# Gathers that convert float32 rows to float16 on the way, in place of a ScalarE cast, in a gather, cumulative-sum and matmul kernel

## The chip, the cores and the metric

The kernel runs on one core of a Trainium2 chip. The metric is the device time of one execution in microseconds (us); medians of several executions are quoted, and fast runs are compared with fast runs. The kernel before takes 349.65 us in the median (348.95 to 350.15, 4 runs).

## The reference, cut to what matters

```python
B, S, N, D = (16, 4096, 2048, 512)        # x: (B, S, D) float32, indices: (B, N) sorted, w: (D, D)
gathered = x[b_idx, indices, :].copy()
cs = np.cumsum(gathered, axis=1)
return np.matmul(cs, w).astype(np.float32)
```

16 x 2048 gathered rows of 2 KB are 67.1 MB read, the output is 67.1 MB written. The kernel works in 256 tiles of 128 rows. For each tile TensorE multiplies the gathered rows with a triangle of ones (the sums, turned so that D, the length of a row, lies on the partitions), VectorE adds the last column of the tile before (the carry), TensorE multiplies with w (the projection), ScalarE drains PSUM to SBUF, and SyncE stores four tiles (1 MB) at a time.

## The kernel before

Gathers are issued by GpSimd, one tile each, into a ring of 16 float32 slots. ScalarE casts them to float16 into a second ring (8 pairs), up to 6 tiles ahead of the drains, and in between drains the projections:

```python
    def gather(t):
        g, r = divmod(t, R)
        if t >= NG:                                        # NG = 16 slots; freed by the casts
            pool.need(s_c, cast_by[R * (g + 1) - NG - 1])
        ...
        nc.gpsimd.indirect_dma_start(
            out=g32[g % (NG // R)][:, r, :],               # float32 slot
            out_offset=None,
            in_=x_flat,
            in_offset=bass.IndirectOffsetOnAxis(ap=ap, axis=0),
            element_offset=(t // NT) * S * D,
        ).then_inc(s_g[t % NG], 16)

    def cast(t, n, first=None):                            # ScalarE
        g, r = divmod(t, R)
        for u in range(t, t + n):
            act.need(s_g[u % NG], 16 * (u // NG + 1), first)
        nc.scalar.copy(
            out=g16[g % NH][:, r : r + n], in_=g32[g % (NG // R)][:, r : r + n]
        ).then_inc(s_c, 1)

    def sums(t, u, first=None):                            # TensorE
        ...
        pe.need(s_c, cast_by[t] if first is None else cast_by[2 * U + t] - 2 * U // R, first)
        ...
            mm = nc.tensor.matmul(
                out=pa[t % NA][:, c],
                lhsT=g16[g % NH][:, r, c * P : (c + 1) * P],
                rhs=uq[:] if first is None and g in PLAIN else ut[:],
                start=(c == 0), stop=(c == DC - 1),
            )
    ...
    def step(u, first=None):                               # ScalarE's program
        ...
        for t, n in casts[u if first is None else 2 * U + u]:
            cast(t if first is None else t - 2 * U, n, first)
        drain(u, first)
```

Of the kernel before, what the change touches and what calls it, by code (L numbers as in the profile page):

```python
# [7 lines left out]
P = 128  # L8
FP32 = mybir.dt.float32
FP16 = mybir.dt.float16  # L10
# [23 lines left out]
def kernel(  # L34
# [7 lines left out]
    nc = tc.nc  # L42

    B, S, D = x.shape
    N = indices.shape[1]
    R = 2
# [3 lines left out]
    T = B * NT  # L50
    G = T // R
# [1 line left out]
    KI = T // P  # L53
    FIRST = 2 * R
    NG = 16
    LEAD = 3
    FAR = 6
    NH = 8
    NA = 4
    NB = 4  # L60
    NC = 4
    W = 2
    H = 1
    NO = 4
    U = NT
    V = max(U, W * R * NO)
    assert V % U == 0 and V % (W * R * NO) == 0 and T % V == 0 and U % NG == 0 and U % NA == 0 and U % (R * NC) == 0 and U % NB == 0
    assert D == 512 and N % (R * P) == 0 and T % P == 0

    x_flat = x.rearrange("b s d -> (b s) d")  # L70
# [1 line left out]
    const = ctx.enter_context(tc.tile_pool(name="const", bufs=1))  # L72
# [8 lines left out]
    ut = const.tile([P, R, Q], FP16)  # L81
    uq = const.tile([P, P], FP16)
    ident = const.tile([P, P], FP32)
    zeros = const.tile([P, D], FP16)
    spare = const.tile([P, 1], FP16)
    g32 = [const.tile([P, R, D], FP32, name=f"g32_{i}") for i in range(NG // R)]
    g16 = [const.tile([P, R, D], FP16, name=f"g16_{i}") for i in range(NH)]
    cst = [const.tile([P, DC, R, P], FP16, name=f"cst{i}") for i in range(NC)]
    ob = [const.tile([P, W, R, D], FP32, name=f"ob{i}") for i in range(NO)]
    pa = [ps.tile([P, DC, R, Q], FP32, name=f"pa{i}") for i in range(NA)]  # L90
# [4 lines left out]
    def sem(name):  # L95
        return tc.alloc_semaphore(name)

    s_z, s_ut, s_wc, s_if, s_pt, s_prep, s_of, s_c = (
        sem(f"s_{n}") for n in ("z", "ut", "wc", "if", "pt", "prep", "of", "c")
    )  # L100
# [1 line left out]
    s_w = [sem(f"s_w{c}") for c in range(DC)]  # L102
    s_idx = [sem(f"s_idx{k}") for k in range(KI)]
    s_ol = sem("s_ol")
    s_g = [sem(f"s_g{i}") for i in range(NG)]
    s_o = [sem(f"s_o{i}") for i in range(NO)]
    s_a = sem("s_a")
    s_d = sem("s_d")
    s_b = sem("s_b")
    s_e = sem("s_e")  # L110

    pool, pe, dve, act, sp = (
        Lane(e) for e in (nc.gpsimd, nc.tensor, nc.vector, nc.scalar, nc.sync)
    )

    casts = []
    cast_by = []
    for u in range(T):
        far = min(FAR, 2 if u < R else 3 + (u + 4) // 8, 3 + (T - 1 - u) // 6)
        casts.append([])  # L120
        while len(cast_by) <= min(u + far, T - 1):
            n = R if far > 5 and len(cast_by) % R == 0 else 1
            casts[u].append((len(cast_by), n))
            cast_by += [cast_by[-1] + 1 if cast_by else 1] * n

    for u in range(2 * U + U, T - 2 * U):
        assert casts[u] == [(t + U, n) for t, n in casts[u - U]]

    def gather(t):
        g, r = divmod(t, R)  # L130
        if t >= NG:
            pool.need(s_c, cast_by[R * (g + 1) - NG - 1])
        if t < FIRST:
            pool.need(s_first[g], 16)
            ap = idx_first[:, t, 0:1]
        else:
            pool.need(s_prep, t // P + 1)
            ap = idxg[:, t // P, t % P : t % P + 1]
        nc.gpsimd.indirect_dma_start(  # L139
            out=g32[g % (NG // R)][:, r, :],  # L140
            out_offset=None,
            in_=x_flat,
            in_offset=bass.IndirectOffsetOnAxis(ap=ap, axis=0),
            element_offset=(t // NT) * S * D,
        ).then_inc(s_g[t % NG], 16)


    PLAIN = (0, 1, G - 2, G - 1)

    def cast(t, n, first=None):  # L150
        g, r = divmod(t, R)
        for u in range(t, t + n):
            act.need(s_g[u % NG], 16 * (u // NG + 1), first)
        nc.scalar.copy(  # L154
            out=g16[g % NH][:, r : r + n], in_=g32[g % (NG // R)][:, r : r + n]
        ).then_inc(s_c, 1)

    def sums(t, u, first=None):
        g, r = divmod(t, R)
        tiles = None if first is None else R * first  # L160
        pe.need(s_c, cast_by[t] if first is None else cast_by[2 * U + t] - 2 * U // R, first)
        pe.need(s_d, t - NA + 1, tiles)
        for c in range(DC):
            if c == 1 and u is not None:
                pe.need(s_e, u - NB + 1, tiles)
            mm = nc.tensor.matmul(  # L166
                out=pa[t % NA][:, c],
                lhsT=g16[g % NH][:, r, c * P : (c + 1) * P],
                rhs=uq[:] if first is None and g in PLAIN else ut[:],
                start=(c == 0),  # L170
                stop=(c == DC - 1),
            )
        mm.then_inc(s_a, 1)
# [28 lines left out]
    def project(u, t, first=None):  # L202
        g, j = divmod(u, R)
        tiles = None if first is None else R * first
        pe.need(s_e, u - NB + 1, tiles)
        pe.need(s_d, u + 1 if first is None and g in PLAIN else R * (g + 1), tiles)
        for c in range(DC):
            if c == 2 and t is not None:
                pe.need(s_d, t - NA + 1, tiles)
            mm = nc.tensor.matmul(  # L210
                out=pb[u % NB][:],
                lhsT=cst[g % NC][:, c, j, :],
                rhs=w16[:, c, :],
                start=(c == 0),
                stop=(c == DC - 1),
            )
        mm.then_inc(s_b, 1)
# [6 lines left out]
    def store(g, n):  # L224
        b, h = divmod(g, GB)
        rows = out[b, h * R * P : (h + n) * R * P, :]
        src = ob[g // W % NO]
        if g in (0, G - 1):
            for j in range(R):
                sp.need(s_e, R * g + j + 1)  # L230
                nc.sync.dma_start(
                    out=rows[j * P : (j + 1) * P, :], in_=src[:, g % W, j]
                ).then_inc(s_ol if g else (s_o[0], s_of)[j >= H], 16)
            return
        sp.need(s_e, R * (g + n))
        order = "(g j p) d -> p g j d" if g in PLAIN else "(g p j) d -> p g j d"
        rows = rows.rearrange(order, p=P, j=R)
        src = src[:, g % W : g % W + n]
        if n < W:
            done = s_ol if g >= W else (s_o[0], s_of)[R + g > H]  # L240
            nc.sync.dma_start(out=rows, in_=src).then_inc(done, 16)
            return
        for i in range(H):
            part = slice(i * P // H, (i + 1) * P // H)
            nc.sync.dma_start(out=rows[part], in_=src[part]).then_inc(s_o[g // W % NO], 16)


    with nc.allow_non_contiguous_dma(reason="a few indices, one per partition"):
        for k, eng in enumerate((nc.sync, nc.scalar)):
            t = k * R  # L250
            eng.dma_start(
                out=idx_first[:, t : t + R, :],
                in_=indices[0, t * P : (t + R) * P]
# [4 lines left out]
    for k in range(KI):  # L258
        nc.sync.dma_start(
            out=idx64[:, k, :], in_=idx_rows[k * P : (k + 1) * P, :]  # L260
# [8 lines left out]
    for g in range(G - W, G):  # L269
        store(g, 1)  # L270
    for i in range(G // W - NO, G // W - 1):
        sp.need(s_o[i % NO], 16 * H * (i // NO + 1))
    sp.need(s_ol, 16 * (R + W - 1))


# [4 lines left out]
        out=ident[:],  # L280
        in_=ident[:],
# [7 lines left out]
        out=ut[:],  # L289
        in_=ut[:],  # L290
# [9 lines left out]
        out=uq[:],  # L300
        in_=uq[:],
# [23 lines left out]
    for k in range(KI):  # L325
# [3 lines left out]
            out=pb[k % NB][:, :P], in_=idxf[:, k, :], identity=ident[:]  # L329
# [20 lines left out]
    order = []  # L350
    done = 0
# [7 lines left out]

    head = order.index((False, 2 * U - 1)) + 1  # L360
    tail = order.index((False, T - 2 * U - 1)) + 1
    step = 2 * U
    for i in range(head + step, tail):
        assert order[i] == (order[i - step][0], order[i - step][1] + U)

    def run(i, first=None):
        is_sums, t = order[i]
        after = next((v for k, v in order[i + 1 :] if k != is_sums), None)
        if first is not None:
            t -= 2 * U  # L370
            after -= 2 * U
        if is_sums:
            sums(t, after, first)
        else:
            pe.need(s_wc, DC)
            project(t, after, first)

    for i in range(head):
        run(i)
    with nc.tensor.Fori(2 * U // R, (T - 2 * U) // R, U // R) as first:  # L380
        pe.new_pass()
        for i in range(head, head + step):
            run(i, first)
# [7 lines left out]
        act.need(s_w[c], 16)  # L391
        nc.scalar.copy(out=w16[:, c, :], in_=w32[:, c, :]).then_inc(s_wc, 1)  # L392
    def step(u, first=None):
        if first is None and u == min(W * R * NO, 2 * U - 1):
            act.need(s_of, 16 * (R + W - 1 - H))
        if u % (W * R) == 0:
            stored = first if first is None else first * (16 * H) // (R * W * NO)
            act.need(s_o[u // R // W % NO], 16 * H * (u // R // W // NO), stored)
        for t, n in casts[u if first is None else 2 * U + u]:
            cast(t if first is None else t - 2 * U, n, first)  # L400
        drain(u, first)


    for u in range(2 * U):
        step(u)
    with nc.scalar.Fori(2 * U, T - 2 * U, V) as first:
        act.new_pass()
        for u in range(V):
            step(u, first)
    for u in range(T - 2 * U, T):  # L410
        step(u)
# [30 lines left out]
```

## Time and profile before

| | us |
|---|---|
| kernel before, timed, median of 4 runs | 349.65 |
| span of the profile that the prediction had | 439.2 |
| span of a second profile of the same kernel, taken later on another execution | 348.4 |

The profile was of an execution that took a quarter longer than the timed ones. A busy row of the page gives an engine's busy time and share; the DMA row gives, in tenths, how busy the 16 DMA engines were in each fortieth of the span; a queue's share is the time of its packets over 16 engines' span.

### The profile page before, as it was taken

Reading aid. Unit: us, or ns where it says so; the run is one execution under the profiler, and the core shown is the slowest. Engines: PE = TensorE matmul, PEld = TensorE weight load, DVE = VectorE, ACT = ScalarE, POOL = GpSimd, SP = SyncE. Lnnn points to the kernel's source line nnn. Section 1 sums busy time; section 2 is a strip of 40 time slices with the busy share of each in tenths; the row PEclk is TensorE's granted clock in tenths of the full one; section 3 lists DMA queues with packets and bytes.
Section 4 is the critical chain, followed back from the end, with each engine's and each line's share of the span. In section 5 each row is a group of like instructions: output and inputs, shape, how many; then the busy total and the mean of one; then the engine's idle time right before and its main releaser. Section 6 shows DMA issues by size and latency. Waiting matters only on the chain.

```text
span 439.2 us, 6408 instructions
## 1 busy us (share of the span) xinstructions
PE 329.8 (75%) x2066; PEld 171.5 (39%) x2066; DVE 178.4 (41%) x263; ACT 263.6 (60%) x407; POOL 243.7 (55%) x266
## 2 busy tenths in 40 slices
PE   6518687777877786679787697768777697876995
PEld 2203343343434343335344353434334343443552
DVE  2104343444344444345344344344345353543552
ACT  4216566556665665576656575566576666665794
POOL 6764557565655566556565465565555665655300
PEclk9756989798989899988899698996989969998898
DMA  7864979799888999989898899988989999999966
GB/s 225 256 212 156 347 273 344 252 336 364 285 318 304 333 351 328 350 294 339 316 353 295 310 336 335 359 318 273 366 310 328 331 337 328 300 330 349 331 242 241
DMA packets 39884, 135.68 MB, mean 309 GB/s; under 512 B 5825, under 2 KB 6081, under 8 KB 39873
## 3 DMA queue, kind: packets, MB, share of 16 engines
q0 software_dynamic: 20480, 67.13, 47.9%
q1 hardware_dynamic: 18832, 67.90, 38.9%
q10 hardware_dynamic: 560, 0.53, 0.4%
q8 instruction: 5, 0.08, 0.1%
q14 instruction: 7, 0.05, 0.0%
HBM read 68.42 MB, written 67.11 MB: 309 GB/s over the span
## 4 chain that ended last, share of the span: by engine, by line
PE 74%; issue 10%; DVE 7%; another core or an unknown queue 7%; ACT 1%; DVEq 0%; ACTq 0%; SPq 0%
PE pb L210 55%; PE pa L166 18%; DVE cst L198 7%; PE pb L316 1%; DVE cst L185 0%; ACT ob L222 0%; ACT g L154 0%; PE pb L328 0%; DVEq L26 0%; DVE zeros L320 0%; DVEq L437 0%; ACTq L26 0%; SPq L93 0%
## 5 line engine op out<-in xcount | busy, mean ns | idle before, releaser
L210 PE MATMUL pb<-w,cst 128*128 128x512 f16 x1024 | 293.1, 414 | 84.7 <-DVE cst L198 60.1
L139 POOL DMA_INDIRECT g<-in_x_dram,idxg x252 | 238.2, 945 | 165.1 <-ACT g L154 97.6
L198 DVE TENSOR_TENSOR cst<-pa,cst 128x512 f16<-128x512 f32 x240 | 166.1, 692 | 231.3 <-PE pa L166 162.2
L222 ACT COPY ob<-pb 128x512 f32<-128x512 f32 x256 | 146.2, 591 | 164.6 <-PE pb L210 108.1
L210 PEld LDWEIGHTS pb<-w,cst 128*128 128x128 f16 x1024 | 94.3, 104 | 164.9 <-DVE cst L198 65.8
L154 ACT CAST g<-g 128x1024 f16<-128x1024 f32 (+1 forms) x147 | 138.4, 945 | 0.3 <-issue 0.2
L166 PE MATMUL pa<-ut,g 128*128 128x128 f16 x992 | 103.9, 230 | 16.0 <-issue 12.8
L166 PEld LDWEIGHTS pa<-ut,g 128*128 128x128 f16 x992 | 81.5, 104 | 87.7 <-issue 33.8
L185 DVE CAST cst<-pa 128x512 f16<-128x512 f32 x16 | 11.0, 686 | 16.2 <-PE pa L166 12.6
L316 PE MATMUL pb<-zeros 128*128 128x512 f16 x16 | 5.9, 538 | 1.5 <-DVE zeros L320 1.5
L139 POOL DMA_INDIRECT g<-in_x_dram,idx_first x4 | 4.0, 994 | 1.6 <-issue 0.9
L166 PE MATMUL pa<-uq,g 128*128 128x128 f16 x32 | 3.1, 219 | 1.9 <-issue 1.8
L166 PEld LDWEIGHTS pa<-uq,g 128*128 128x128 f16 x32 | 2.2, 97 | 4.2 <-issue 3.1
L316 PEld LDWEIGHTS pb<-zeros 128*128 128x128 f16 x16 | 2.1, 135 | 4.2 <-issue 2.2
L392 ACT CAST w<-w 128x512 f16<-128x512 f32 x2 | 1.1, 616 | 3.4 <-DMA w<-in_w_dram 3.4
L389 ACT ACT_TABLE_LOAD x1 | 1.3, 1283 | 2.5 <-issue 2.5
L323 DVE CAST idxf<-idx 128x128 f32<-128x128 uint32 x2 | 0.5, 227 | 3.8 <-DMA idx<-in_indices_dram 3.8
L337 DVE CAST w<-w 128x512 f16<-128x512 f32 x2 | 0.8, 422 | 1.6 <-DMA w<-in_w_dram 1.6
L328 PE MATMUL pb<-ident,idxf 128*128 128x128 f32 x2 | 0.9, 447 | 0.0
L328 PEld LDWEIGHTS pb<-ident,idxf 128*128 128x128 f32 x2 | 0.4, 206 | 0.9 <-issue 0.9
L320 DVE MEMSET zeros<- 128x256 uint32 x1 | 0.3, 272 | 1.1 <-SPq L93 1.1
L334 DVE CAST idxg<-pb 128x128 uint32<-128x128 f32 x2 | 0.6, 292 | 0.3 <-PE pb L328 0.2
(11 smaller groups left out, 2.1 us busy)
## 6 DMA issues: line engine op xcount, KB each, us to landing
out_dram<-ob SPq DMA_DIRECT2D x62, 1024.0 KB
g<-in_x_dram,idxg POOLq DMA_INDIRECT x252
out_dram<-ob SPq DMA_DIRECT2D x4, 256.0 KB, 2.8
out_dram<-ob SPq DMA_DIRECT2D x2, 512.0 KB, 3.4
w<-in_w_dram ACTq DMA_DIRECT2D x2, 256.0 KB, 3.3
w<-in_w_dram SPq DMA_DIRECT2D x2, 256.0 KB
idx<-in_indices_dram SPq DMA_DIRECT2D x2, 128.0 KB, 2.6
g<-in_x_dram,idx_first POOLq DMA_INDIRECT x4
```

Source lines behind the costliest of these rows:

```text
L139: nc.gpsimd.indirect_dma_start(out=g32[g % (NG // R)][:, r, :], out_offset=None, in_=x_flat, in_offset=bass.IndirectOffsetOnAxis(ap=ap, ax ...
L154: nc.scalar.copy(out=g16[g % NH][:, r : r + n], in_=g32[g % (NG // R)][:, r : r + n]).then_inc(s_c, 1)
L166: mm = nc.tensor.matmul(out=pa[t % NA][:, c], lhsT=g16[g % NH][:, r, c * P : (c + 1) * P], rhs=uq[:] if first is None and g in PLAIN else ...
L185: nc.vector.tensor_copy(out=dst, in_=src).then_inc(s_d, 1)
L198: nc.vector.tensor_tensor(out=dst, in0=src, in1=last, op=mybir.AluOpType.add).then_inc(s_d, 1)
L210: mm = nc.tensor.matmul(out=pb[u % NB][:], lhsT=cst[g % NC][:, c, j, :], rhs=w16[:, c, :], start=(c == 0), stop=(c == DC - 1),)
L222: nc.scalar.copy(out=ob[g // W % NO][:, g % W, j], in_=pb[u % NB][:]).then_inc(s_e, 1)
L316: nc.tensor.matmul(out=pb[NB - 1][:], lhsT=zeros[:, :P], rhs=zeros[:], start=True, stop=True)
L328: nc.tensor.transpose(out=pb[k % NB][:, :P], in_=idxf[:, k, :], identity=ident[:]).then_inc(s_pt, 1)
L337: nc.vector.tensor_copy(out=w16[:, c, :], in_=w32[:, c, :]).then_inc(s_wc, 1)
L389: nc.scalar.copy(out=spare[:], in_=zeros[:, :1])
L392: nc.scalar.copy(out=w16[:, c, :], in_=w32[:, c, :]).then_inc(s_wc, 1)
```

## The change

The intent is to take the cast off ScalarE: GpSimd's gathers write float16 directly, the sums read the gathers' slots, and the slots are freed by the sums. The core of the diff (the rest reworks how waits are counted in TensorE's loop, which is now 32 tiles long, and strips parameters whose value was 1):

```diff
-    LEAD = 3
-    FAR = 6
-    NH = 8
+    NS = 32
+    FREE = 2
+    LEAD = 4
...
-    g32 = [const.tile([P, R, D], FP32, name=f"g32_{i}") for i in range(NG // R)]
-    g16 = [const.tile([P, R, D], FP16, name=f"g16_{i}") for i in range(NH)]
+    g16 = [const.tile([P, R, D], FP16, name=f"g16_{i}") for i in range(NG // R)]
...
-        if t >= NG:
-            pool.need(s_c, cast_by[R * (g + 1) - NG - 1])
+        if t % FREE == 0:
+            pool.need(s_a, t + FREE - NG)
...
-            out=g32[g % (NG // R)][:, r, :],
+            out=g16[g % (NG // R)][:, r, :],
...
-    def cast(t, n, first=None):
-        ...
-        pe.need(s_c, cast_by[t] if first is None else cast_by[2 * U + t] - 2 * U // R, first)
+        pe.need(s_g[t % NS], 16 * (t // NS + 1) - skip // R, first)
...
-                lhsT=g16[g % NH][:, r, c * P : (c + 1) * P],
+                lhsT=g16[g % (NG // R)][:, r, c * P : (c + 1) * P],
...
-        for t, n in casts[u if first is None else 2 * U + u]:
-            cast(t if first is None else t - 2 * U, n, first)
         drain(u, first)
```

More of the change, by code (lines that the diff above doesn't have):

```diff
@@ L62 @@
     W = 2
-    H = 1
     NO = 4
     U = NT
-    V = max(U, W * R * NO)
-    assert V % U == 0 and V % (W * R * NO) == 0 and T % V == 0 and U % NG == 0 and U % NA == 0 and U % (R * NC) == 0 and U % NB == 0
+    V = NS
+    assert V % NS == 0 and NS % NG == 0 and FREE == R and NS == 16 * R and 2 * U % NS == 0 and (T - 4 * U) % V == 0 and U % (W * R * NO) == 0 and U % NA == 0 and U % (R * NC) == 0 and U % NB == 0
     assert D == 512 and N % (R * P) == 0 and T % P == 0
@@ L104 @@
     s_ol = sem("s_ol")
-    s_g = [sem(f"s_g{i}") for i in range(NG)]
+    s_g = [sem(f"s_g{i}") for i in range(NS)]
     s_o = [sem(f"s_o{i}") for i in range(NO)]
@@ L114 @@
     )
-    casts = []
-    cast_by = []
-    for u in range(T):
-        far = min(FAR, 2 if u < R else 3 + (u + 4) // 8, 3 + (T - 1 - u) // 6)
-        casts.append([])
-        while len(cast_by) <= min(u + far, T - 1):
-            n = R if far > 5 and len(cast_by) % R == 0 else 1
-            casts[u].append((len(cast_by), n))
-            cast_by += [cast_by[-1] + 1 if cast_by else 1] * n
-    for u in range(2 * U + U, T - 2 * U):
-        assert casts[u] == [(t + U, n) for t, n in casts[u - U]]
     def gather(t):
         g, r = divmod(t, R)
-        if t >= NG:
-            pool.need(s_c, cast_by[R * (g + 1) - NG - 1])
+        if t % FREE == 0:
+            pool.need(s_a, t + FREE - NG)
         if t < FIRST:
@@ L144, in gather @@
             element_offset=(t // NT) * S * D,
-        ).then_inc(s_g[t % NG], 16)
+        ).then_inc(s_g[t % NS], 16)
     PLAIN = (0, 1, G - 2, G - 1)
-    def cast(t, n, first=None):
-        g, r = divmod(t, R)
-        for u in range(t, t + n):
-            act.need(s_g[u % NG], 16 * (u // NG + 1), first)
-        nc.scalar.copy(
-            out=g16[g % NH][:, r : r + n], in_=g32[g % (NG // R)][:, r : r + n]
-        ).then_inc(s_c, 1)
     def sums(t, u, first=None):
@@ L160, in sums @@
         tiles = None if first is None else R * first
-        pe.need(s_c, cast_by[t] if first is None else cast_by[2 * U + t] - 2 * U // R, first)
-        pe.need(s_d, t - NA + 1, tiles)
+        skip = 0 if first is None else 2 * U
+        pe.need(s_g[t % NS], 16 * (t // NS + 1) - skip // R, first)
+        pe.need(s_d, t - NA + 1 - skip, tiles)
         for c in range(DC):
             if c == 1 and u is not None:
-                pe.need(s_e, u - NB + 1, tiles)
+                pe.need(s_e, u - NB + 1 - skip, tiles)
             mm = nc.tensor.matmul(
                 out=pa[t % NA][:, c],
-                lhsT=g16[g % NH][:, r, c * P : (c + 1) * P],
-                rhs=uq[:] if first is None and g in PLAIN else ut[:],
+                lhsT=g16[g % (NG // R)][:, r, c * P : (c + 1) * P],
+                rhs=uq[:] if g in PLAIN else ut[:],
                 start=(c == 0),
@@ L204, in project @@
         tiles = None if first is None else R * first
-        pe.need(s_e, u - NB + 1, tiles)
-        pe.need(s_d, u + 1 if first is None and g in PLAIN else R * (g + 1), tiles)
+        skip = 0 if first is None else 2 * U
+        pe.need(s_e, u - NB + 1 - skip, tiles)
+        pe.need(s_d, (u + 1 if g in PLAIN else R * (g + 1)) - skip, tiles)
         for c in range(DC):
             if c == 2 and t is not None:
-                pe.need(s_d, t - NA + 1, tiles)
+                pe.need(s_d, t - NA + 1 - skip, tiles)
             mm = nc.tensor.matmul(
@@ L230, in store @@
                 sp.need(s_e, R * g + j + 1)
+                done = s_ol if g else (s_o[0], s_of)[j]
                 nc.sync.dma_start(
                     out=rows[j * P : (j + 1) * P, :], in_=src[:, g % W, j]
-                ).then_inc(s_ol if g else (s_o[0], s_of)[j >= H], 16)
+                ).then_inc(done, 16)
             return
         sp.need(s_e, R * (g + n))
-        order = "(g j p) d -> p g j d" if g in PLAIN else "(g p j) d -> p g j d"
-        rows = rows.rearrange(order, p=P, j=R)
-        src = src[:, g % W : g % W + n]
-        if n < W:
-            done = s_ol if g >= W else (s_o[0], s_of)[R + g > H]
-            nc.sync.dma_start(out=rows, in_=src).then_inc(done, 16)
-            return
-        for i in range(H):
-            part = slice(i * P // H, (i + 1) * P // H)
-            nc.sync.dma_start(out=rows[part], in_=src[part]).then_inc(s_o[g // W % NO], 16)
+        done = {1: s_of, G - W: s_ol}.get(g, s_o[g // W % NO])
+        nc.sync.dma_start(
+            out=rows.rearrange(
+                "(g j p) d -> p g j d" if g in PLAIN else "(g p j) d -> p g j d", p=P, j=R
+            ),
+            in_=src[:, g % W : g % W + n],
+        ).then_inc(done, 16)
     with nc.allow_non_contiguous_dma(reason="a few indices, one per partition"):
@@ L271 @@
     for i in range(G // W - NO, G // W - 1):
-        sp.need(s_o[i % NO], 16 * H * (i // NO + 1))
+        sp.need(s_o[i % NO], 16 * (i // NO + 1))
     sp.need(s_ol, 16 * (R + W - 1))
@@ L361 @@
     tail = order.index((False, T - 2 * U - 1)) + 1
-    step = 2 * U
+    step = 2 * V
     for i in range(head + step, tail):
-        assert order[i] == (order[i - step][0], order[i - step][1] + U)
+        assert order[i] == (order[i - step][0], order[i - step][1] + V)
     def run(i, first=None):
@@ L368, in run @@
         after = next((v for k, v in order[i + 1 :] if k != is_sums), None)
-        if first is not None:
-            t -= 2 * U
-            after -= 2 * U
         if is_sums:
@@ L379 @@
         run(i)
-    with nc.tensor.Fori(2 * U // R, (T - 2 * U) // R, U // R) as first:
+    with nc.tensor.Fori(2 * U // R, (T - 2 * U) // R, V // R) as first:
         pe.new_pass()
@@ L393, in step @@
     def step(u, first=None):
-        if first is None and u == min(W * R * NO, 2 * U - 1):
-            act.need(s_of, 16 * (R + W - 1 - H))
         if u % (W * R) == 0:
-            stored = first if first is None else first * (16 * H) // (R * W * NO)
-            act.need(s_o[u // R // W % NO], 16 * H * (u // R // W // NO), stored)
-        for t, n in casts[u if first is None else 2 * U + u]:
-            cast(t if first is None else t - 2 * U, n, first)
+            if first is None and u == W * R * NO:
+                act.need(s_of, 16 * (R + W - 2))
+            act.need(s_o[u // R // W % NO], 16 * (u // R // W // NO), first)
         drain(u, first)
@@ L405 @@
         step(u)
-    with nc.scalar.Fori(2 * U, T - 2 * U, V) as first:
+    with nc.scalar.Fori(2 * U, T - 2 * U, U) as first:
         act.new_pass()
-        for u in range(V):
+        for u in range(U):
             step(u, first)
```

## The prediction

> **What bounds the kernel now.** I read the page first (span, busy shares, slices, queues), then the groups of instructions by form, then the waits of GpSimd, and last the timeline of GpSimd in the middle of the run. The unprofiled time is 349.82 us (349.49 to 350.15); the profiled execution took 439.2 us, so the profile stretches this kernel by a quarter and I use its durations and its order of waits, not its span.
>
> From the page of the kernel before (engine busy time, slices of the span, DMA queues as packets, MB and share of the time of 16 engines):
>
> ```profile
> PE 329.8 (75%) x2066; PEld 171.5 (39%) x2066; DVE 178.4 (41%) x263; ACT 263.6 (60%) x407; POOL 243.7 (55%) x266
> ...
> DMA  7864979799888999989898899988989999999966
> ...
> q0 software_dynamic: 20480, 67.13, 47.9%
> q1 hardware_dynamic: 18832, 67.90, 38.9%
> ```
>
> No engine is full, while the DMA row stands at 8 and 9 tenths from the fifth slice nearly to the end. The two big queues, gathers (q0) and stores (q1), add to 86.8% of 439.2 us, that is 381 us per DMA engine: more than the whole unprofiled time, so the profiled packets are slower than the unprofiled ones. In the packet records a gather packet carries 4096 bytes (two rows of 2 KB) and took 159 ns in the median (mean 203, with a tail), a store packet of 4096 bytes 159 ns in the median too (mean 164). With the median everywhere, one engine has 1024 gather packets and 992 such store packets: 2016 x 159 ns = 320.5 us, and about 11 us for 96 packets of 2 KB and the small ones. That is **a DMA floor of some 332 us** for an unprofiled time of 349.82, plus about 4 us before the first gather and 3 us for the last store to land: 339 us. The DMA engines are the first bound.
>
> The groups by form, then the waits of GpSimd, then its timeline (start, duration, instruction, in brackets the idle time before it and what ended it):
>
> ```profile
> L210 PE MATMUL pb<-w,cst 128*128 128x512 f16 x1024 | 293.1, 414 | 84.7 <-DVE cst L198 60.1 <-issue 24.4
> L139 POOL DMA_INDIRECT g<-in_x_dram,idxg x252 | 238.2, 945 | 165.1 <-ACT g L154 97.6 <-issue 67.4
> ...
> L222 ACT COPY ob<-pb 128x512 f32<-128x512 f32 x256 | 146.2, 591 | 164.6 <-PE pb L210 108.1 <-remote 46.2 <-issue 10.1
> L154 ACT CAST g<-g 128x1024 f16<-128x1024 f32 x109 | 115.2, 1057 | 0.0
> ...
> L154 ACT CAST g<-g 128x512 f16<-128x512 f32 x38 | 23.4, 623 | 0.3 <-issue 0.2
> ```
>
> ```profile
> POOL g L139 <- ACT g L154: 97.6, 42, 5.1
> POOL g L139 <- issue: 68.4, 213, 1.2
> ```
>
> ```profile
> 206.98 0.95 POOL L139 DMA_INDIRECT g<-in_x_dram,idxg  x1 [0.30 <-issue]
> 208.23 0.95 POOL L139 DMA_INDIRECT g<-in_x_dram,idxg  x1 [0.30 <-issue]
> 209.48 0.95 POOL L139 DMA_INDIRECT g<-in_x_dram,idxg  x1 [0.30 <-issue]
> 213.72 0.94 POOL L139 DMA_INDIRECT g<-in_x_dram,idxg  x1 [3.29 <-ACT g L154]
> ```
>
> The reader is to see a **second bound close behind the first**: even with nothing to wait for, GpSimd starts a gather only every 1.25 us (208.23 - 206.98), so 256 gathers take 320 us. The first starts at 3.2 us; from the last sums to the end of the span took 7.6 us (431.6 to 439.2), and a landing takes about 3 us (the small stores landed in 2.8 to 3.4). That makes a **GpSimd floor of 3 + 320 + 3 + 8 = 334 us**. The 97.6 us for which GpSimd waited for ScalarE's casts are not ScalarE's own work: they come in bursts (3.29 us before the gather at 213.72), where ScalarE itself had waited for a gather to land ("remote", 46.2 us). The ring of 16 float32 slots is full of gathers in flight.
>
> TensorE is third: in a warm stretch of the timeline the sums of successive tiles start 1.09 us apart (423.13, 424.22), 256 x 1.09 = 279 us. ScalarE is no better: two drains and a cast of a pair, 2 x 0.591 + 1.057 = 2.24 us per pair, 287 us in all.
>
> **What the Trainium skill says.** "DMA: Bandwidth & Descriptors", section "SWDGE vs HWDGE vs iDMA", gives a cast during a DMA to transfers issued from GpSimd alone; the gathers here are already issued there, so the change is open to them. It gives no rate for a casting transfer, and the trace of the kernel before has none: that is the great unknown. The same page, "Where 436 GB/s comes from", puts the fabric's ceiling at 435 GB/s; 4096 bytes in 159 ns on 16 engines are 412 GB/s here, and 134.2 MB of x and output over 349.82 us are 384 GB/s, so the trace agrees that little is left. "Perfetto Trace Analysis", section "DMA Instruction — SWDGE (GPSIMD)", says that the profiled end of such an instruction is the end of descriptor generation, not of the data's movement; the trace agrees, with 945 ns for every gather while the landings come several microseconds later. "TensorE: Matmul & The Clock Gate", Part 1, says that an idle window halves the array's clock; the trace agrees: four 512-column matmuls take 1.03 us warm and 1.71 to 1.89 us after a wait for data.
>
> **The change part by part.**
>
> - ScalarE loses 147 casts, 115.2 + 23.4 = 138.6 us, and keeps 256 drains, about 150 us. ScalarE goes from 287 us of work to 150. Not on the path by itself: worth 0 directly. Indirectly the drains no longer stand behind a cast that waits for a gather, so PSUM buffers come free on time. I guess 1 to 4 us of smoother flow.
> - At each end one cast leaves the path between landing and first sums: 2 x 0.62 = 1.2 us.
> - SBUF writes of the gathers halve (67.1 to 33.6 MB); reads from HBM and the stores stay. If a packet is paced by what it reads, 159 ns for 4096 bytes stays and the DMA floor is still 332 us. If it is paced by what it writes, the gathers' 1024 packets fall from 163 to about 81 us per engine, the floor falls to 250 us, and GpSimd's 334 us become the bound.
> - GpSimd issues the same 256 gathers. If generating the descriptors with a conversion costs more, each extra 0.1 us is 25.6 us on an engine that has only 349.8 - 334 = 16 us of slack.
> - The ring has 16 slots as before, but a slot is freed by the sums on TensorE (a pair at a time) and not by a cast; the 8 float16 pairs behind it disappear. As sums start when a gather has landed, and TensorE at 1.09 us is faster than the tiles come (349.8 / 256 = 1.37 us), a slot is held perhaps 1 us longer, against 16 x 1.37 = 22 us for a turn of the ring. Cost 0 to 3 us. The larger lead of the sums, 4 tiles for 3, balances part of it.
> - TensorE's instruction count is unchanged; VectorE and the stores are unchanged in size and number.
>
> Sum for the middle case: 349.8 - 1.2 (casts at the ends) - about 3 (coupling) + about 1 (later slots) = 346.6 if the packets are as fast as before; 334 + 3 = 337 if converting packets are shorter and only GpSimd binds.
>
> **The rivals.**
>
> 1. The transfer is hidden anyway: DMA time is read-bound, the halved write is worth nothing, and the freed ScalarE was never the bound. For it: stores and gathers both take 159 ns for 4 KB, and both read 4 KB. Against it: gather packets have a tail (mean 203), which may lie on the write side. It makes 344 to 349 us.
> 2. GpSimd's issue becomes the bound at its old pace: 335 to 340 us. For it: 1.25 us is the pace wherever the ring lets it run. This needs shorter or steadier gather packets.
> 3. Conversion costs: descriptor generation above 945 ns, or packets over 159 ns. 10% on the gather packets alone is 16 us of DMA (365 us), 10% on the descriptors (0.095 x 256 = 24 us, less 16 of slack) some 358. A halved conversion rate would be 163 us more. Nothing in the profile speaks for or against it; the care with which the slots, leads and semaphores of the changed kernel are set up suggests to me that it is not drastic.
> 4. TensorE waits straight on gathers, with no float16 buffer between, cools and slows: 1.03 to 1.8 us for a group of four. For it: the granted clock is 0.892 in the profile already. Against it: at 1.09 of 1.37 us a tile it is busy 80%. A few us at most.
>
> **Range and chances.** I give rival 1 four chances in ten, rival 2 nearly four, rival 3 something under two. The middle of the first two is 342; the range reaches from just under the GpSimd floor to a conversion cost of about 10%: 332 to 362. Faster by over 2% means under 342.8, which takes in rival 2 and a lucky part of rival 1: 0.47. Within 2%: 0.36. Slower: 0.17.
>
> **What would show each step right or wrong.** In the changed profile: the gathers' duration on GpSimd (945 ns if descriptors cost the same) and their spacing (1.25 us when nothing holds them); the share of q0 (47.9% of 439.2 us is 210 us: about the same if read-bound, far less if write-bound, more if conversion is slow); ScalarE's busy time near 150 us; GpSimd waiting for sums where it waited for casts, with less than 97.6 us if GpSimd is now the bound; TensorE's mean clock near 0.89 or above. A gather duration or a q0 share well above those of before would make the prediction wrong, as would a wait of GpSimd for the sums that is longer than the one for the casts.

## The result, and the profile after

The changed kernel takes **354.69 us** in the median (354.58 to 355.12, 4 runs), against 349.65 before: a ratio of 1.0148, 95% interval 1.0128 to 1.0168. (Ratios here are the mean time of one kernel's fast runs over that of the other's of the same rounds, so not quite the ratio of the medians quoted.) The sign is the other way round from the forecast: 1.5% slower, not 2% faster. That is under 2%, but the interval lies clear of 1.

The page of the changed kernel (its span is 352.9 us; this execution is not stretched):

```profile
PE 303.1 (86%) x2066; PEld 152.3 (43%) x2066; DVE 179.1 (51%) x263; ACT 152.4 (43%) x260; POOL 242.0 (69%) x266
...
DMA  7999999999999999999999999999999999999996
...
q0 software_dynamic: 36864, 33.57, 58.8%
q1 hardware_dynamic: 18832, 67.90, 50.3%
```

ScalarE is at 152.4 us, as expected. But the gathers' queue has 36,864 packets where it had 20,480, for half the bytes written, and its packets take 58.8% of 352.9 us, 207.5 us per DMA engine. The two queues together take 109% of the span, so the recorded times of packets overlap on an engine.

The groups of instructions and the waits of the changed kernel that answer to those shown of before (total idle time, number, longest), and three successive gathers on GpSimd:

```profile
L124 POOL DMA_INDIRECT g<-in_x_dram,idxg x252 | 236.6, 939 | 82.1 <-issue 61.3
...
L201 ACT COPY ob<-pb 128x512 f32<-128x512 f32 x256 | 149.8, 585 | 190.3 <-PE pb L189 190.3
```

```profile
PEld pa L144 <- DMA g<-in_x_dram,idxg: 89.3, 111, 1.8
POOL g L124 <- issue: 62.3, 204, 0.3
PE pa L144 <- DMA g<-in_x_dram,idxg: 40.2, 72, 1.3
POOL g L124 <- PE pa L144: 20.8, 51, 1.3
```

```profile
201.20 0.94 POOL L124 DMA_INDIRECT g<-in_x_dram,idxg  x1 [0.30 <-issue]
202.45 0.94 POOL L124 DMA_INDIRECT g<-in_x_dram,idxg  x1 [0.30 <-issue]
203.69 0.94 POOL L124 DMA_INDIRECT g<-in_x_dram,idxg  x1 [0.30 <-issue]
```

Descriptors that convert cost GpSimd no more: 939 ns on the mean, one gather every 1.24 us. The sums now wait straight for gathers to land. So the question is whether the gathers come later because the DMA engines need longer for them, because the ring frees later, or because GpSimd's pace binds.

### The profile page after: what moved, and what is told of

The parts are those of the page before. It is cut to its first block, busy times and chain, and to the rows that moved or that the text cites. A ratio compares the mean times of both kernels' runs of the same rounds, so it can differ in the third digit from the quotient of the medians.

```text
span 352.9 us, 6040 instructions
## 1 busy us (share of the span) xinstructions
PE 303.1 (86%) x2066; PEld 152.3 (43%) x2066; DVE 179.1 (51%) x263; ACT 152.4 (43%) x260; POOL 242.0 (69%) x266
## 3 DMA queue, kind: packets, MB, share of 16 engines
q0 software_dynamic: 36864, 33.57, 58.8%
## 4 chain that ended last, share of the span: by engine, by line
DMA 61%; POOL 18%; PE 12%; issue 7%; POOLq 0%; ACT 0%; SPq 0%
DMA g<-in_x_dram,idxg 61%; POOL g L124 18%; PE pb L189 8%; PE pa L144 4%; DMA idx_first<-in_indices_dram 1%; POOLq L287 0%; ACT ob L201 0%; SPq L408 0%; SPq L91 0%
## 5 line engine op out<-in xcount | busy, mean ns | idle before, releaser
L189 PE MATMUL pb<-w,cst 128*128 128x512 f16 x1024 | 262.3, 379 | 1.1 <-DVE cst L176 0.6
L201 ACT COPY ob<-pb 128x512 f32<-128x512 f32 x256 | 149.8, 585 | 190.3 <-PE pb L189 190.3
L144 PE MATMUL pa<-ut,g 128*128 128x128 f16 x992 | 97.0, 220 | 39.9 <-DMA g<-in_x_dram,idxg 38.9
L144 PEld LDWEIGHTS pa<-ut,g 128*128 128x128 f16 x992 | 68.3, 98 | 121.3 <-DMA g<-in_x_dram,idxg 86.6
L189 PEld LDWEIGHTS pb<-w,cst 128*128 128x128 f16 x1024 | 89.5, 98 | 63.0 <-issue 1.2
L293 PE MATMUL pb<-zeros 128*128 128x512 f16 x16 | 7.2, 632 | 1.5 <-DVE zeros L297 1.5
```

What stands on the lines that cost most here:

```text
L144: mm = nc.tensor.matmul(out=pa[t % NA][:, c], lhsT=g16[g % (NG // R)][:, r, c * P : (c + 1) * P], rhs=uq[:] if g in PLAIN else ut[:], star ...
L189: mm = nc.tensor.matmul(out=pb[u % NB][:], lhsT=cst[g % NC][:, c, j, :], rhs=w16[:, c, :], start=(c == 0), stop=(c == DC - 1),)
L201: nc.scalar.copy(out=ob[g // W % NO][:, g % W, j], in_=pb[u % NB][:]).then_inc(s_e, 1)
L293: nc.tensor.matmul(out=pb[NB - 1][:], lhsT=zeros[:, :P], rhs=zeros[:], start=True, stop=True)
```

## The experiments

Three theories go through the expectations. **A**: the converting packets cost the DMA engines more. **B**: the ring, freed by the sums, is too short. **C**: GpSimd's pace of 1.24 us a gather binds. Each kernel is an edit of the changed one unless said otherwise, and the diffs show the core of each edit. Packet durations below are from the packet records of each trace.

### The kernel before once more

> The kernel before, unchanged, for a second profile beside the others. Its first profiled execution took 439.2 us where its timed ones took 349.7, while the changed kernel's profile was not stretched (352.9 for 354.7). If the stretch is the profiler's doing, it comes again (420 to 450 us). If it was a disturbed execution, this one is near 350 us, with gather packets of 4 KB near 159 ns in the mean and a DMA row at 9 throughout.

Measured: 350.09 us, span 348.4. The page of this profile, and GpSimd's waits:

```profile
DMA  7799999999999999999999999999999999999975
...
q0 software_dynamic: 20480, 67.13, 49.9%
q1 hardware_dynamic: 18832, 67.90, 48.3%
```

```profile
POOL g L139 <- issue: 70.7, 232, 0.3
...
POOL g L139 <- ACT g L154: 7.0, 23, 0.3
```

The DMA row is full from the third slice on, and 98% of the span is packet time. GpSimd never waits longer than the 0.3 us that lies between any two gathers: its last gather starts at 322.4 us, within 0.5 us of where 3.2 + 255 x 1.25 us puts it. The 97.6 us of waiting in the first profile belong to the stretched execution alone. So the stretch is not the profiler's doing. On the chip of the very last runs below, the kernel before took 436 to 444 us in all 7 timed runs, at granted TensorE clocks of 0.89 to 0.91, like the 0.892 of the first profile; so the first profile probably fell on such a chip. What is different there, the chip or where the data lie, is open.

The number of drains in a fixed stretch shows the pace. The two profiles, before and then changed, as stretches of time (from and to, length, ScalarE's busy time on drains and their count, granted clock, DMA share, GB/s):

```profile
0.00:56.00 56.00, 16.48 (x30) 0.97 0.91 317
56.00:331.00 275.00, 116.28 (x218) 1.00 1.02 413
```

```profile
0.00:56.00 56.00, 18.14 (x31) 1.00 1.02 237
56.00:331.00 275.00, 123.00 (x211) 1.00 1.13 301
```

The counts of this view include a drain that only reaches over an edge. By their starts in the trace, the kernel before drains 216 tiles in the 275 us (1.273 us each), the changed one 211 (1.303). So at 331 us the kernel before has 10 tiles left and the changed one 14, though it had been one ahead at 56 us. The ends then take 17.4 and 21.9 us, and the 4.5 us between them are the difference of the spans, 352.9 - 348.4: the loss is built up in the steady stretch. GB/s counts what is written, so 301 and 413 can't be compared; a share over 1 is packets that overlap.

### Conversion alone, in the kernel before

```diff
-    g32 = [const.tile([P, R, D], FP32, name=f"g32_{i}") for i in range(NG // R)]
+    g32 = [const.tile([P, R, D], FP16, name=f"g32_{i}") for i in range(NG // R)]
```

> The kernel before with one thing changed: the gathers convert to float16 on the way, and ScalarE still copies every tile (float16 to float16), with the old slots, leads and waits. Result correct. Theory A (the converting packets cost the DMA engines more: 98 ns per 2 KB row for 79.5): slower than before, 354 to 362 us, as the DMA engines are the bound. Theory B (conversion is harmless; slots freed by the sums instead of by casts hold the gathers back): like before, 345 to 351 us.

Measured: 355.58 us (354.66 to 356.59), correct, ratio 1.0150 (1.0128 to 1.0173) to before. The same two lines of this kernel:

```profile
q0 software_dynamic: 36864, 33.57, 58.7%
q1 hardware_dynamic: 18832, 67.90, 50.1%
```

```profile
56.00:331.00 275.00, 111.22 (x209) 1.00 1.13 299
```

With all of the old scheme kept, slots freed by casts and ScalarE as busy as before, converting gathers alone make the whole loss. Theory B is out as its cause, and the picture of the queues is that of the changed kernel.

### Twice the slots

```diff
-    NG = 16
+    NG = 32
```

> The changed kernel with 32 slots for 16. Theory A (DMA packets bind): same as changed within 0.7%, 352 to 355 us, gathers only wait longer in the queue. Theory B (the ring is too short for gathers that take 14.2 us from issue to landing): clearly faster, 340 to 347 us, and GpSimd's 20.8 us of waits for the sums gone. Theory C (GpSimd's pace of 1.24 us binds): GpSimd's waits gone, and the time falls by at most these 20 us, to about 335.

Measured: 354.75 us (353.97 to 356.06), ratio to before 1.0136 (1.0112 to 1.0159); 212 tiles in the stretch for 211. GpSimd's real waits disappear:

```profile
POOL g L124 <- PE pa L144: 9.8, 32, 0.3
```

Nothing is longer than 0.3 us now, and it gains nothing. The gathers of the kernel before (second profile) and of this one, with the first and last start:

```profile
L139 POOL DMA_INDIRECT g<-in_x_dram,idxg x252: 942/946/1187, 8.4 to 322.4; - x126
```

```profile
L124 POOL DMA_INDIRECT g<-in_x_dram,idxg x252: 936/937/1062, 8.3 to 320.6; - x126
```

With 32 slots the last gather starts at 320.6 us, earlier than in the kernel before (322.4) and than in the changed kernel (325.8), and the span still ends 5 us after that of the kernel before (353.4 for 348.4). So neither the ring (B) nor GpSimd's pace (C) sets the end; the gathers wait in the DMA queue, up to 25.4 us from issue to landing for 20.8 in the changed kernel.

### No conversion and no cast

```diff
-    g16 = [const.tile([P, R, D], FP16, name=f"g16_{i}") for i in range(NG // R)]
+    g16 = [const.tile([P, R, D], FP32, name=f"g16_{i}") for i in range(NG // R)]
...
-                lhsT=g16[g % (NG // R)][:, r, c * P : (c + 1) * P],
+                lhsT=g16[g % (NG // R)][:, r, c * P : (c + 1) * P].bitcast(BF16)[:, 1::2],
```

(The triangles of ones become bfloat16.)

> The changed kernel without conversion and without casts: gathers bring float32 rows into 16 float32 slots, and the sums read the high 16 bits of each element as bfloat16, every second 2-byte word. Less exact on purpose (truncation). Theory A: gather packets of 4 KB at about 159 ns again, DMA floor 332 us, time 335 to 345 us, faster than both kernels. Theory B: the ring is as in the changed kernel, so still 352 to 356 us. If the strided weight loads are slow, TensorE's weight loads will show it (98 ns each in the changed kernel).

Measured: **347.85 us** (347.57 to 348.56), ratio to before 0.9943 (0.9924 to 0.9962), 0.6% faster than the kernel before and 1.9% faster than the changed one. It truncates x to bfloat16 and so is less exact. The expectation of 335 to 345 was too low. Its queues and its stretch:

```profile
q0 software_dynamic: 20480, 67.13, 49.9%
q1 hardware_dynamic: 18832, 67.90, 48.6%
```

```profile
56.00:331.00 275.00, 127.34 (x218) 1.00 1.03 414
```

The same slots, the same leads, the same waits as the changed kernel, and with plain gathers the pace of the kernel before is back. The strided weight loads are harmless (98 ns each). Side by side: taking the cast away, with all else that the new scheme changes, is worth 349.99 - 347.85 = 2.1 us; conversion costs 5.6 us in the old scheme (355.58 - 349.99) and 6.8 us in the new (354.69 - 347.85, the changed kernel being of another job).

### ScalarE's load without its data

```diff
+        act.need(s_i, u - 2, first)
+        nc.scalar.copy(out=idle16[u % 4][:], in_=idle32[:]).then_inc(s_i, 1)
         drain(u, first)
```

(An edit of the kernel without conversion and cast.)

> The kernel high_halves with a cast of 128x512 per tile added on ScalarE, from a constant tile to tiles that nothing reads: ScalarE gets its old load back (256 x about 0.62 us), but no data passes through it. If ScalarE's load was worth nothing, as predicted, 347.5 to 348.8 us as high_halves; if the load itself cost time, 349.5 to 351.

Measured: 348.77 us (348.12 to 349.44), ratio to before 0.9963 (0.9936 to 0.9991). ScalarE is busy for 283.3 us instead of 152.5, and the time is within 1 us of 347.85; the two intervals overlap, so it is no clear difference. ScalarE's load was worth at most about 1 us of the 2.1; what the rest is worth was not parted further.

### More DMA work beside the gathers

```diff
         store(g, W)
+        sp.need(s_x[n % 4], 16 * (n // 4))
+        nc.sync.dma_start(
+            out=ex[n % 4][:], in_=x_flat[n * 1024 : n * 1024 + P, :]
+        ).then_inc(s_x[n % 4], 16)
```

(In the kernel without conversion, and in the changed kernel.)

> The kernel high_halves (plain gathers) with 62 extra loads of 256 KB of x into unused tiles, one behind each large store, 16.3 MB in all, so that the DMA engines and not GpSimd's issue are clearly the bound. 16.3 MB at the 415 GB/s of the steady stretch are 39 us: 380 to 392 us. It is the base for the next run.

> The changed kernel (converting gathers) with the same extra loads. The gap to loaded_plain is the DMA cost of the conversion without GpSimd's pace beside it. If the durations of the packets add up (98 ns for 79.5 per row, 2048 rows an engine), the gap is 30 to 38 us. If the engine works on packets of two queues at once and the steady stretches tell its true cost (a tile every 1.307 us for 1.258), the gap is 10 to 15 us. If only the mixture with GpSimd's issue matters, it stays near the 7 us of the unloaded pair.

Measured: 389.83 us (389.76 to 390.01) plain and 398.18 us (397.12 to 398.45) converting, a gap of 8.35 us. That rules out that packet durations simply add up (30 to 38 us), but lies between the two other bands, so it doesn't decide between them. (The second band took 1.258 us for a tile without conversion. From the 41st drain to the 241st a tile takes 1.277 us in the kernel without conversion and 1.311 in the changed one, 8.8 us for 256 tiles, which would have put that band about where the measurement fell.) The DMA issues with their median time from issue to landing, plain and then converting, show what else happens:

```profile
out_dram<-ob SPq DMA_DIRECT2D x62, 1024.0 KB, 20.9
g<-in_x_dram,idxg POOLq DMA_INDIRECT x252, 7.0
```

```profile
out_dram<-ob SPq DMA_DIRECT2D x62, 1024.0 KB, 8.1
g<-in_x_dram,idxg POOLq DMA_INDIRECT x252, 21.6
```

With plain gathers the stores pile up, with converting gathers the gathers do. An engine that takes turns between queues by the packet would do that, as a turn of the gathers' queue is one row instead of two; this is argued from the landing times, not shown. The plain kernel's last gather starts at 355.8 us of a span of 388.3, and from 366 us its DMA share is only 0.70; that may hide or swell part of the conversion's cost in this comparison.

### Half rows, plain and converting

```diff
-    x_flat = x.rearrange("b s d -> (b s) d")
+    x_flat = x.rearrange("b s (k c) -> (b s k) c", k=2)
...
-            out=g16[g % (NG // R)][:, r, :],
+            out=g16[g % (NG // R)][:, r, : D // 2],
```

(Each with sums over the half that is there; both give a wrong result.)

> The kernel high_halves with gathers of half rows (1 KB each, plain), wrong result on purpose: same number of gathers and rows, half the bytes, so the DMA engines have air and GpSimd's issue alone is the bound. The prediction's GpSimd floor was 334 us: 332 to 337 us here if it was right. Packets of 4 KB with four rows at 159 ns if a plain packet goes by bytes.

> The changed kernel with gathers of half rows that convert (256 float32 read, 512 bytes written), wrong result on purpose: for the packet records. About 49 ns a packet if a converting packet's time goes by its bytes or elements; 75 ns or more if most of the 98 ns is a fixed cost of a packet. The whole time near half_rows (332 to 337 us) if GpSimd is then the bound.

Measured: 338.12 us (338.04 to 338.29) plain, 336.00 us (335.81 to 336.37) converting. Both have as many gathers and half the bytes, and GpSimd, never held, sets the end (338.12 is 1 us above the forecast):

```profile
L125 POOL DMA_INDIRECT g<-in_x_dram,idxg x252: 942/946/1094, 8.4 to 322.2; - x126
```

```profile
L124 POOL DMA_INDIRECT g<-in_x_dram,idxg x252: 936/937/951, 8.3 to 320.4; - x126
```

(Minimum, median and maximum in ns, first and last start.) So the floor of GpSimd is 336 to 338 us, and the kernel before stands only 12 us above it. The converting one is the faster here: with room on the DMA engines (gathers land 3.9 us after issue, 4.3 plain), conversion shows no cost, and its slightly shorter descriptor work (937 for 946 ns) is 256 x 9 ns = 2.3 us. The packet records, in ns (median; a converting packet is recorded with the bytes that it writes, half of those read):

| gather | bytes read per packet | rows | gather packet | store packet of 4 KB |
|---|---|---|---|---|
| plain, 2 KB rows (before) | 4096 | 2 | 159 | 159 |
| plain, 1 KB rows | 4096 | 4 | 159 | 160 |
| converting, 2 KB rows (changed) | 2048 | 1 | 98 | 172 |
| converting, 1 KB rows | 1024 | 1 | 60 | 168 |

The converting packet goes by 38 ns per KB read, just as the plain one does ((98 - 60) ns for one KB more; the plain loads and stores have 46, 84 and 159 ns for 1, 2 and 4 KB). What differs is the part that stays: 22 ns for a converting packet, 8 or 9 for a plain one, and a converting packet never holds more than one row. The 60 ns lie between the two forecasts, 49 and 75: part goes by bytes, part is fixed.

The extra 13 ns are not the converting packet's alone. In the changed kernel 78% of the stores' 4 KB packets took exactly 172 ns and 21% the old 159, and most packets of 4 bytes 22 instead of 9; in the mixture of the next run, 41% of the store packets and 12% of the plain gathers' took 172. What decides which of the plain packets carry it is not shown.

### Every second gather

Even tiles convert, odd tiles are plain and read as bfloat16:

```diff
+        [const.tile([P, D], (FP16, FP32)[r], name=f"g16_{i}_{r}") for r in range(R)]
...
+                lhsT=rows.bitcast(BF16)[:, 1::2] if r else rows,
```

> A mixture: even tiles are gathered with conversion to float16 as in the changed kernel, odd tiles plainly with their high halves read as bfloat16 as in high_halves; everything else as in both. If each converting gather costs its own share of DMA time, the time lies midway between high_halves (347.85) and the changed kernel (354.7): 350.5 to 352. If the cost comes from something that one converting stream in the queue sets off for all packets, it stays near 354.

Measured: 349.56 us (348.49 to 351.76), correct, ratio to before 0.9998 (0.9968 to 1.0027). Its stretch:

```profile
56.00:331.00 275.00, 126.46 (x217) 1.00 1.08 358
```

Half of the conversions cost 1.7 of 6.8 us, a quarter. The cost is not the constant one that a single converting stream would set off, and it looks less than linear; but the intervals of the two ratios leave about 0.7 to 3.1 us, just short of the half (3.4), and the jobs were different ones. It fits two bounds that lie close together, GpSimd at 1.25 us a tile and the DMA engines just above: the first conversions use up what little room there is. That reading is not shown by a run.

### Parting converting from splitting: a miss

> The kernel high_halves with plain gathers of rows of 640 float32 (2560 bytes), so that two rows no longer fit a packet of 4096 bytes; wrong result on purpose, 25% more gathered bytes. It parts the two things that conversion brings at once, packets of one row and the converting itself. If packets of one row are harmless, the steady stretch moves 413 to 416 GB/s as with plain rows of 512 and the time is 383 to 388 us (589,824 bytes a tile at 415 GB/s are 1.42 us, x 256 = 364, and about 22 for start and end). If they are what costs (the 0.045 us a tile that conversion adds, over 8 rows an engine), the stretch moves about 402 GB/s and the time is 394 to 399 us.

The kernel without conversion got rows of 640 elements (`L = 640`, the flat x seen as rows of L). Measured: 388.20 us (386.99 to 388.97), wrong, 415 GB/s in the stretch. The packet records have 16,384 packets of 5120 bytes: still two rows each, so the 4096 bytes that the expectation took for a limit are none here. The run shows that larger plain packets keep the full rate, but it does not part what it was to part.

### One row per packet on both sides

```diff
+    L = 2 * D
+    x_flat = x.rearrange("b s d -> (b s d)").rearrange("(n c) -> n c", c=L)
...
+    g16 = [const.tile([P, R, L], FP32, name=f"g16_{i}") for i in range(NG // R)]
...
+            element_offset=(t // NT) * S * D // 2,
```

(In the kernel without conversion; in the changed kernel the slots stay FP16.)

> The kernel high_halves with plain gathers of rows of 1024 float32 (4096 bytes), wrong result on purpose: one row fills a packet, so this is the plain base for one-row packets. 786,432 bytes a tile at 415 GB/s are 1.895 us, x 256 = 485, and about 20 for start and end: 500 to 510 us, gather packets 159 ns.

> The changed kernel with converting gathers of the same rows of 1024 (4096 bytes read, 2048 written), wrong result on purpose: one row a packet on both sides, so only the converting differs from rows1024_plain. If the extra cost of the changed kernel is that of converting (a fixed 13 ns or so per packet, as half_conv suggests: 22 + 38 ns per KB read), packets take about 174 ns and the time is 5 to 15 us above rows1024_plain. If converting is free and only the splitting into one-row packets cost, packets take 159 ns and the time is within 3 us of rows1024_plain.

Measured: 499.39 us (498.61 to 500.74) plain, 503.55 us (502.98 to 503.92) converting, both wrong; the same job, so 4.2 us apart. All 32,768 gather packets hold one row on both sides, and take 159 ns plain and 172 ns converting. So a packet takes 13 ns more when it converts (14 with 1 or 2 KB read: 60 for 46, 98 for 84), and 86% of the store packets beside it take 172 ns as well. The gap is a little below the band of 5 to 15 us, and just outside the 3 us of "free": neither forecast was met. The changed kernel has the same number of gather packets; so of its 6.8 us perhaps 4 are for converting as such, and the rest, some 2 to 3 us, is left for packets of one row in place of two. This split is an estimate: the two runs have other bytes per tile, and they fell on the chip where the kernel before took 436 to 444 us (these two do not look disturbed: 418 GB/s in the plain one's stretch, and gather packets of 161 ns in the mean, where the first profile had 203).

## Why the prediction was wrong

- **The DMA engines are the first bound.** Right, but closer than thought: undisturbed, the kernel before has its DMA row full and 98% of the span in packets, and it drains a tile every 1.273 us where GpSimd issues one every 1.25. The floor of 332 us was mis-sized, because it took the median of 159 ns for every packet: the recorded packets of the two queues come to 342 us (98.2% of 348.4), and without any conversion or cast the kernel still takes 347.85. So there was little above the floor to be won.
- **A packet is paced by what it reads, or by what it writes.** This step failed. The middle case lets 4096 bytes read take 159 ns at most, "if the packets are as fast as before"; longer packets were left to rival 3, with "something under two" chances in ten. The read side was right: a packet goes by 38 ns per KB read, and no gain from the halved write shows. Missing was the fixed part: 13 ns more for a packet, and twice as many packets, as two rows no longer share one. For 4096 bytes read that is 2 x 98 = 196 ns in place of 159. That conversion in the gathers costs the time is shown (5.6 us alone in the old scheme, none with half rows); how the 5 to 7 us divide between the two parts is only estimated.
- **"10% on the gather packets alone is 16 us of DMA."** Mis-sized in the other direction. The converting packets took 203.3 us per engine where the undisturbed kernel before had 171.5, 19% more, and the stores' 4 KB packets 168.0 for 159.6; together 40 us more. The time rose by 5 to 7 us. Recorded packets overlap (a DMA share of 1.13 in the stretch), and their durations don't add up to occupancy. So rival 3 was the one that came true, and its price, 16 us for 10%, was too high.
- **GpSimd's floor of 334 us, and no extra cost for its descriptors.** Nearly right: 336 to 338 us measured, 939 ns for 945. It did not come to bind, since the step before it failed. That the sum came so close is in part luck: its tail of 7.6 us is from the stretched profile.
- **ScalarE's 138.6 us are worth 0 directly, 1 to 4 us in all with the smoother flow.** A guess by its own word, and right in size: taking the cast away gave 2.1 us, of which the load as such is at most about 1.
- **Slots freed by the sums cost 0 to 3 us.** Right, and rather 0: twice the slots gained nothing.
- **TensorE cools without a buffer (rival 4).** Not seen: a granted clock of 0.999. The 0.892 that spoke for it belonged to the stretched execution, as did the waits of GpSimd for casts. (The reading "1.71 to 1.89 us after a wait" is also loose: at 213.41 us of that trace the group right after a wait of 2.71 us took 1.04, the next two 1.74 and 1.84.)
- **The signs named in advance.** They would have missed it. The gathers' duration (939 for 945 ns) and GpSimd's waits for the sums (20.8 us for 97.6) came out as hoped, and q0 took 207.5 us per engine, "about the same" as the 210 of the stretched profile. Only against the undisturbed 173.9 us (49.9% of 348.4) does the 19% show.

The gain that was expected is there, 2 us. It is outweighed by a cost on the resource that was already full, and which no line of the profile before could show, as it had no converting packet.

## What to carry to other kernels

An operation that is moved from an engine with room into a transfer need not be free: where the DMA engines bind, count packets and what stays fixed per packet, not bytes alone, and measure the packet of the new kind before building a scheme around it. With room on the DMA engines (half rows) conversion showed no cost. And when a profile's span doesn't fit the timed runs, take another one before reading its waits.

## What the Trainium skill lacked or had wrong

- "DMA: Bandwidth & Descriptors", section "SWDGE vs HWDGE vs iDMA", says who may cast during a DMA but gives no cost. Here a gather packet that converts took 13 ns more than a plain one of the same size (172 for 159 ns with 4 KB read), and held one row where plain ones held two; conversion alone, put into the kernel before, made it 1.5% slower.
- The same section calls a packet "≤4096 B preferably". Plain gather packets here were filled with whole rows up to 4096 bytes or just over: four rows of 1 KB, two of 2 KB, but also two of 2560 bytes (5120). Converting ones held a single row, even of 1 KB.
- I found no page with the pace of indirect gathers: 128 rows every 1.24 to 1.25 us (0.94 us of descriptors and 0.30 between), which puts a floor of 336 to 338 us under these kernels.
- Nor one that says by how much recorded packet durations overlap on an engine: they came to 1.02 to 1.13 times the stretch in kernels whose DMA engines were full.
- I found no page that explains a chip on which the same kernel takes 436 to 444 us instead of 349 to 352; why is open.
